# Other orders at three places of a hybrid decoder layer: a token norm and two weight splits, the rows of W_out, and a transpose's bank

## The chip, the cores and the metric

The kernel runs on one core of one Trainium2 chip. The time is the device time of one execution in microseconds (us); lower is better. Several executions are taken of each kernel, and their median counts. One more execution is recorded by the hardware profiler; all views of the trace come from it.

The engines are named as in the profile: PE is the matrix engine (TensorE; PEld its weight loads), DVE is VectorE, ACT is ScalarE, POOL is GpSimd, and SP issues the loads and stores. L1265 is line 1265 of the kernel.

## The reference

One decoder layer on 1024 tokens of width 1024 in float32, with 16 learned meta tokens ahead of them (so L = 1040 positions). The mixer has two groups of heads side by side, a state-space part (SSD) and a stick-breaking attention; a gated feed-forward part with a short convolution follows. Cut to what matters here:

```python
proj = rms_norm(h, mix_pre_g) @ w_in             # z, xbc (X, B, C), dt, q, k, v
y_ssd = ssd_mixer(z, xbc, dt_raw, ...)           # uses B and C, chunk by chunk
# stick breaking, per head: beta = sigmoid(q.k / 8)
w = beta[t, s] * prod(1 - beta[t, j] for s < j < t)
y_sb = rms_norm(w @ v, sb_norm_g)
mix = concatenate([y_ssd, y_sb], -1) @ w_out
h = h + rms_norm(mix, mix_post_g)
gu = rms_norm(h, ffn_pre_g) @ w_up               # g and u, 2816 columns each
f = (gelu(causal_dwconv(gu[..., :D_FF])) * gu[..., D_FF:]) @ w_down
h = h + rms_norm(f, ffn_post_g)
```

## The kernel before

**Products.** A float32 product is made of three: each operand is split into a rounded high part (`hi`, an ACT copy to `F32R`) and the rest (`lo`, a subtraction on POOL or DVE), and hi x hi, lo x hi and hi x lo are added up in PSUM. The order of the three differs: where weights are split against x (`plain`, L1336) it is weight-hi with x-hi, weight-hi with x-lo, then weight-lo with x-hi.

**Stages.** First the input norm, the projections and the SSD scan. Then the attention, eight pairs of heads `p` with eight blocks `i` of 128 queries; between its pieces PE gets the remaining projections and, at the end, the first half of W_out's product, as filling. Then the second half of W_out's product, token block by token block, with each block's two norms. Then the feed-forward products (`Problem`; `g0` and `u0` are the first two), in a scheme with seven products for eight, and last the product with W_down.

**What sets the order.** Outside of marked regions a planner orders each engine's instructions by its own estimates when the program is built; a region `manual_schedule` keeps the order of the code for the engines it names. Through the attention only PE is in such a region, so ACT, DVE, POOL and SP are the planner's there. From the second token block of W_out's second half to the end, PE, DVE, ACT and POOL all keep the order of the code (`ORDERED`), and SP is the planner's. `tc.issue_after(ins)` adds an edge of order alone: what its block emits on `ins`'s engine comes behind `ins` there. Tiles of one tag share a number of buffers (`bufs`), and a new tile waits until a buffer of its tag is free.

**Attention, one block (p, i).** `block_weights` (L752) computes the scores in chunks: PE writes a chunk to a tile `zz` (z), ACT reads it twice, into `kp` (L773) and `bt` (L774), both by a sigmoid. DVE scans `kp` (L780), POOL multiplies it into `bt` (L782). Two blocks later `block_turn` turns `bt` with PE (tw, L794), also into a tile `zz`, and ACT copies that to `th` (L796); `block_mix` (L809) is the product with v. There are two `zz` buffers for z and tw together. The loop gives PE the order: z, mix of an earlier block, filling, the turn of a block two back, filling.

**W_out's rows.** `wout_steps` (L888) prepares eight rows of W_out's first half, one per call: the raw row is loaded (tag `wraw`, two buffers), ACT copies it with a gain to the high part (`woa`, L894), DVE makes the rest (L895). `STAGE` says how many rows are to be there after block (p, i): one after (6,2), and one more per block up to eight after (7,1); the room for them comes from the projected x as the last projections end. `split_y` (L945) splits a block of the SSD's output the same way (yh on ACT, L951; yl, L952). In the trace, row six stands ahead of the score copies of block (6,6), though its call is at the end of block (6,7); the eight rows run from 776.5 to 822.8 us.

**B in token order.** `to_tokens` (L472) turns a 128-channel strip of X or B to token order in three parts: part 0 has the 16 meta tokens, parts 1 and 2 have four blocks of 128 each. Each part is written to a `tp` bank and copied out by DVE. There are two `tp` banks in this stage, and two `sd` banks, which the SSD scan uses.

**The last token block.** `after` (L1160) is the pair of norms of one token block, a generator with four stops: Square on ACT (L1162) and the root on POOL (ms, rs, L191 and L192) | scale and residual on DVE (L1165, L1166) and a store | second Square (L1171) | second root | and at its end the normed block `oxn` (DVE, L1175), which PE turns (x2tp, L1181). For block 8 the stops are spread by hand over the first feed-forward products. Their operands are g0's and u0's weights: `split_w` (L1262) splits a raw tile into `whi` (ACT, L1264) and `wlo` (POOL, L1265). PE's order there is: g0's first strip with x's first half (`ga_`) | x2tp of block 7 | `ga_`'s second half | g0's second strip with the first half (`gb_`, operands `whi2g` and `wlo2g`) | u0's first strip (`ua_`) | x2tp of block 8 | `gb_`'s second half | the rest.

The calls that the change touches there, before it:

```python
        elif t == NT:                      # L1511, ahead of the loop's end
            g0_pair = pair_w("2g0")
            u0.split_1()
            g0.split_2(g0_pair)
            load_raw(1, 1, wp, "wraw", 2)
...
    ga_ = g0_first(0, ("a11", "a12"))      # L1566
    run(ga_, 1)
    run(norm, 2)
    split_b22(nc.vector)
    turn7 = turn_x2(7, P, xn7, x2_tiles(7))
```

Of the kernel before, what the change touches and what calls it, by code (L numbers as in the profile page):

```python
# [9 lines left out]
F32 = mybir.dt.float32  # L10
F32R = mybir.dt.float32r
BF16 = mybir.dt.bfloat16
AF = mybir.ActivationFunctionType
ALU = mybir.AluOpType
# [3 lines left out]
P = 128  # L18
# [13 lines left out]
QSCALE = 0.125  # L32
# [9 lines left out]
WB = 3  # L42
# [11 lines left out]
def tile_layer(ctx: ExitStack, tc: tile.TileContext, x, meta, rows, parts,  # L54
               w_z, w_xbc, w_dt, w_q, w_k, w_v, w_out, w_up, w_down, out):
    nc = tc.nc
# [3 lines left out]
    wp = ctx.enter_context(tc.tile_pool(name="weights", bufs=2, side="left"))  # L60
# [13 lines left out]
    def psum_sd(name):  # L74
        return stage[0][1].tile([P, 512], F32, tag="sd", name=name, bufs=2)
# [10 lines left out]
    def psum_tp(name):  # L86
        return stage[0][1].tile([P, 4, P], F32, tag="tp", name=name, bufs=tp_bufs[0])
# [82 lines left out]
    def run(steps, n=None):  # L170
        for _ in steps if n is None else zip(range(n), steps):
            pass
# [55 lines left out]
    with tc.tile_pool(name="pre", bufs=3, side="right") as pre, \  # L228
# [21 lines left out]
        raws = {"B0": raw_of("B0", w_xbc[8])}  # L250
# [62 lines left out]
        for i in range(NT + 1):  # L313
# [7 lines left out]
            if i == 1:  # L321
                hl = wp.tile([P, KB, 32], F32R, tag="whi", name="wh_dt", bufs=WB)
# [42 lines left out]
    left = [0, 0]  # L365
# [87 lines left out]
    with tc.tile_pool(name="ssd", bufs=1, side="right") as sp:  # L453
# [17 lines left out]

        def to_tokens(src, dst, nm):  # L472
            for part in range(3):
                tp = psum_tp(f"tt_{nm}_{part}")
                if part == 0:
                    nc.tensor.transpose(tp[:NM, 0, :], src[:, 0:NM], ident)
                    nc.vector.tensor_copy(dst[:NM, 0, :], tp[:NM, 0, :])
                else:
                    for b in range(4):
                        t = 4 * (part - 1) + b  # L480
                        nc.tensor.transpose(tp[:, b, :], src[:, NM + t * P:NM + (t + 1) * P], ident)
                    nc.vector.tensor_copy(dst[:, 1 + 4 * (part - 1):5 + 4 * (part - 1), :], tp)
# [269 lines left out]
    def block_weights(p, i):  # L752
        kh, kl = heads[p][1]
        nm = f"{p}_{i}"
        if (p, i) not in qsplit:
            split_q(p, i)
        qh, ql = qsplit.pop((p, i))
        if i == 0:
            edges[p] = ap.tile([P, 2, NT, NM], F32, tag="cb", name=f"cb{p}", bufs=2)
            nc.gpsimd.memset(edges[p][:, :, :, NM - 1:], 0.0)  # L760
        n = NM + (i + 1) * P
        kpt = ap.tile([P, 2, L], F32, tag="kp", name=f"kp{nm}", bufs=2)
        btt = ap.tile([P, 2, L], F32, tag="bt", name=f"bt{nm}", bufs=3)
        kp, bt = kpt[:, :, 0:n], btt[:, :, 0:n]
        chunks = key_chunks(n)
        for ci, (a, w) in enumerate(chunks):
            if ci == 2:
                yield
            z = psum_zz(f"z{nm}_{ci}")
            for s_, (u, r) in enumerate(((qh, kh), (ql, kh), (qh, kl))):  # L770
                for h, j in zip(halves, range(2)):
                    mm(z[:, j, :w], u[h, :], r[h, a:a + w], start=s_ == 0, stop=s_ == 2)  # L772
            nc.scalar.activation(kp[:, :, a:a + w], z[:, :, :w], AF.Sigmoid, scale=-QSCALE)  # L773
            nc.scalar.activation(bt[:, :, a:a + w], z[:, :, :w], AF.Sigmoid, scale=QSCALE)  # L774
        nxt = (p, i + 1) if i < NT - 1 else (p + 1, 0)
        if nxt[0] in heads:
            split_q(*nxt)
        m = n - NM
        for j in range(2):
            nc.vector.tensor_tensor_scan(kp[:, j][:, ::-1], kp[:, j][:, ::-1], hold[:, L - n:L][:, ::-1], 0.0,  # L780
                                         op0=ALU.mult, op1=ALU.max)
            nc.gpsimd.tensor_tensor(bt[:, j, 0:m], bt[:, j, 0:m], kp[:, j, 1:m + 1], op=ALU.mult)  # L782
        nc.gpsimd.tensor_tensor(edges[p][:, :, i, 0:NM - 1], bt[:, :, m:n - 1], kp[:, :, m + 1:n], op=ALU.mult)
        turn.append((p, i, bt))
# [160 lines left out]
    def split_y(pool, half, t, tags, yk=None, eng=nc.gpsimd):  # L945
        nm = f"{half}_{t}"
        if yk is None:
            yk = load_y(half, t, yraw[0](f"yk{nm}"))
        yh = pool.tile([P, 8, P], F32R, tag=tags[0], name=f"yh{nm}", bufs=tags[2])
        yl = pool.tile([P, 8, P], F32R, tag=tags[1], name=f"yl{nm}", bufs=tags[2])  # L950
        nc.scalar.activation(yh, yk, AF.Copy)  # L951
        eng.tensor_tensor(yl, yk, yh.bitcast(F32), op=ALU.subtract)  # L952
        return yh, yl
# [43 lines left out]
    meta_steps = attend_meta()  # L997
    first = wsteps = None
    ys1 = []
    pe_order = ExitStack()  # L1000
    pe_order.enter_context(tc.manual_schedule(engines={mybir.EngineType.PE}))
    FILL = (3, 2, 1, 1, 1, 1, 1, 0)
    STAGE = {(6, 2): 1, (6, 3): 2, (6, 4): 3, (6, 5): 4, (6, 6): 5, (6, 7): 6, (7, 0): 7, (7, 1): 8}
    for p in range(8):
        for i in range(NT):
            if p == 0 and i == 0:
                run(fill, 1)
            block = block_weights(p, i)
            next(block, None)
            if mix:  # L1010
                block_mix(*mix.pop(0))
            if p > 0 and p != 6 and i == 3:
                edge_mix(p - 1, edge)
            run(fill, 1 + (i < FILL[p]))
            if p == 6 and i == 3:
                edge_mix(p - 1, edge)
            if first:
                run(first, 1)
            run(block)
            if (p, i) == (7, 1):  # L1020
                halo = halo_rows(ap, 0, y0a, wres, psum_mm("halo0"))
                run(halo, 3)
            ahead = iter(())
            if len(turn) > 2:
                ahead = begin_turn()
            if (p, i) == (7, 1):
                run(halo, 2)
            if i < NT - 1:
                run(ahead)
            run(fill, int(p > 0 or i > 3))  # L1030
            if (p, i) == (7, NT - 1):
                run(first, 1)
            run(ahead)
            if left[0] and wsteps is None:
                wres = []
                wsteps = wout_steps(third_slots(), 0, ssd_g, wres, [])
                y0a = halo_y(ap, 0)
            if (p, i) == (6, 3):
                yk = [load_y(0, 1, rp.tile([P, L + 3], F32, tag="rq", name="yk0_1", bufs=3)[:, :D]
                             .rearrange("p (a b) -> p a b", b=P)),  # L1040
                      load_y(0, 2, rp.tile([P, L], F32R, tag="rk", name="yk0_2", bufs=3).bitcast(F32)[:, :D]
                             .rearrange("p (a b) -> p a b", b=P))]
            if left[1] and not ys1:
                ys1.append(split_y(wp, 0, 1, ("whi", "wlo", WB), yk[0], nc.vector))
            if p > 0 and i == 2:
                edge = edge_turn(p - 1)
            for _ in range(2):
                if wsteps and len(wres) < min(8, 3 * left[0], STAGE.get((p, i), 0)):
                    run(wsteps, 1)
            if wsteps and first is None and len(wres) == 8:  # L1050
                run(wsteps)
                first = ssd_half(wres, ys1)
                run(first, 1)
                ys1.append(split_y(wp, 0, 2, ("whi", "wlo", WB), yk[1], nc.vector))
            elif first:
                run(halo)
                run(first, 1)
            if p == 7 and 2 < i < 6:
                run(meta_steps, 1)
            if p == 0 and i == 2:  # L1060
                token_rstd(r_ssd, ap, "a")
# [190 lines left out]
    raws = {}  # L1252

    def load_raw(j, gu, pool, tag, bufs):
        r = pool.tile([P, KB, P], F32, tag=tag, name=f"wr{gu}{j}", bufs=bufs)
        nc.sync.dma_start(out=r, in_=w_up[j, gu])
        raws[gu, j] = r

    def pair_w(nm):
        return [wp.tile([P, KB, P], F32R, tag=f"w{e}", name=f"w{e}{nm}", bufs=WB) for e in ("hi", "lo")]  # L1260
# [205 lines left out]
    for t in range(1, NT + 1):  # L1466
# [41 lines left out]
        if t == 7:  # L1508
            g0.split_1()
            load_raw(0, 1, wp, "wraw", 2)  # L1510
        elif t == NT:  # L1511
            g0_pair = pair_w("2g0")
            u0.split_1()
            g0.split_2(g0_pair)
            load_raw(1, 1, wp, "wraw", 2)
        run(steps)
        if t == 6:
            edge_x2()
# [41 lines left out]
    def g0_first(jj, ws):  # L1560
        g = f1.tile([P, 4, 258], F32, tag="gr", name=f"gr0_{jj}", bufs=2)
        g0.g.append(g)
        ghalf.append((g[:, 0:2, :], g[:, 2:4, :]))
        return g0.first_half(ws, psum_fa(f"g0{ws[0]}"), ghalf[jj], part_g)

    ga_ = g0_first(0, ("a11", "a12"))  # L1566
    run(ga_, 1)
    run(norm, 2)
    split_b22(nc.vector)
    turn7 = turn_x2(7, P, xn7, x2_tiles(7))  # L1570
    run(turn7, 1)
    run(norm, 1)
    xn8 = f1.tile([P, 1032], F32, tag="fa", name="oxn8")[:, :D]
    run(norm, 1)
    run(ga_)
    last_norm[0] = xn8
    run(norm)
# [333 lines left out]
```

## Time and profile before

| | us |
|---|---|
| median of 3 executions | 1728.21 (1726.89, 1728.21, 1728.25) |
| the profiled execution's own time | 1726.21 |
| its span, first to last instruction | 1724.3 |
| PE busy in the span | 1703.0 |
| POOL / DVE / ACT busy | 850.4 / 1117.8 / 821.2 |
| mean granted clock of PE | 0.998 |

How to read the views. A timeline row has the start and the duration in us, the engine, the line, the operation, output <- inputs, their shapes and types, how many instructions are merged in it (x1), and in brackets the idle time of the engine ahead of it with what ended that. A row of waits has who waited for whom, the total in us, how often, and the longest. A row of windows has the window, its length, PE's busy time with the instructions begun in it, the granted clock as a share of full speed, the share of the DMA engines and the GB/s. Starts and ends of matmuls overlap, as they are pipelined. A wait for several things is put down to the one that came last by the profile; where that engine had long been done, it was another.

### The profile page before, as it was taken

Reading aid. Unit: us, or ns where it says so; the run is one execution under the profiler, and the core shown is the slowest. Engines: PE = TensorE matmul, PEld = TensorE weight load, DVE = VectorE, ACT = ScalarE, POOL = GpSimd, SP = SyncE. Lnnn points to the kernel's source line nnn. Section 1 sums busy time; section 2 is a strip of 40 time slices with the busy share of each in tenths; the row PEclk is TensorE's granted clock in tenths of the full one; section 3 lists DMA queues with packets and bytes.
Section 4 is the critical chain, followed back from the end, with each engine's and each line's share of the span. In section 5 each row is a group of like instructions: output and inputs, shape, how many; then the busy total and the mean of one; then the engine's idle time right before and its main releaser. Section 6 shows DMA issues by size and latency. Waiting matters only on the chain. (4 is left out here: it accounts for less than half of the span.)

```text
span 1724.3 us, 28047 instructions
## 1 busy us (share of the span) xinstructions
PE 1703.0 (99%) x11230; PEld 1496.2 (87%) x11230; DVE 1117.8 (65%) x1233; ACT 821.2 (48%) x1370; POOL 850.4 (49%) x642
## 2 busy tenths in 40 slices
PE   7999999999999999999999999999999999999998
PEld 6999889888999998998788788999888888887886
DVE  5752973875676677578530567676666666658777
ACT  5423663555566566557652344433333333344544
POOL 4323664585566575565552122587767777400001
PEclk9999999999999999999999999999999999999999
DMA  4233343231011101112214653233332223395334
GB/s 164 58 111 98 105 127 108 68 105 38 26 38 38 36 28 38 38 50 86 64 68 147 212 174 123 73 107 110 103 92 92 92 92 99 118 330 180 105 113 179
DMA packets 90674, 173.87 MB, mean 101 GB/s; under 512 B 10704, under 2 KB 35816, under 8 KB 90544
## 3 DMA queue, kind: packets, MB, share of 16 engines
q1 hardware_dynamic: 90544, 172.08, 31.4%
q8 instruction: 88, 1.44, 0.4%
q14 instruction: 42, 0.34, 0.1%
HBM read 122.32 MB, written 49.73 MB: 100 GB/s over the span
## 5 line engine op out<-in xcount | busy, mean ns | idle before, releaser
L782 POOL TENSOR_TENSOR bt<-bt,kp 128x256 f32<-128x256 f32 (+7 forms) x128 | 213.0, 1683 | 185.7 <-DVE kp L780 144.3
L780 DVE TENSOR_TENSOR_SCAN kp<-kp,hold 128x272 f32<-128x272 f32 (+7 forms) x128 | 183.5, 1474 | 24.7 <-ACT kp L773 14.3
L1265 POOL TENSOR_TENSOR wlo<-wr,whi 128x1024 fp32r<-128x1024 f32 x43 | 107.7, 2516 | 37.8 <-ACT whi L1264 37.8
L1768 POOL TENSOR_TENSOR fms<-fms 128x1 f32<-128x1 f32 x8 | 2.6, 331 | 223.8 <-ACT dh L1653 197.1
L773 ACT ACTIVATE kp<-z 128x288 f32<-128x288 f32 (+6 forms) x112 | 82.6, 737 | 50.5 <-PE z L772 27.8
L1264 ACT ACTIVATE whi<-wr 128x1024 fp32r<-128x1024 f32 x43 | 45.6, 1060 | 111.5 <-PE fX L1322 67.9
L165 PE MATMUL pj_k<-xs,wh_k 128*128 128x400 f32 (+2 forms) x384 | 95.6, 336 | 0.0
L165 PE MATMUL pj_v<-xs,wh_v 128*128 128x400 f32 (+2 forms) x384 | 95.0, 334 | 0.0
L1394 DVE SCALAR_TENSOR_TENSOR ga<-gr,pp,ga 128x1024 f32<-128x1024 f32 x44 | 71.8, 1632 | 35.1 <-ACT ga L1387 34.3
L165 PE MATMUL pj_q<-xs,wh_q 128*128 128x386 f32 (+2 forms) x384 | 93.8, 331 | 0.0
L796 ACT ACTIVATE th<-tw 128x1024 f32<-128x1024 f32 (+2 forms) x96 | 75.6, 815 | 37.4 <-PE tw L794 37.3
L1653 ACT ACTIVATE dh<-ar 128x512 fp32r<-128x512 f32 x77 | 48.6, 631 | 92.9 <-PE dnB L1731 44.7
L165 PE MATMUL pj_X<-xs,wh_X 128*128 128x400 f32 (+2 forms) x384 | 92.0, 326 | 0.0
L165 PE MATMUL pj_z<-xs,wh_z 128*128 128x386 f32 (+2 forms) x384 | 91.6, 326 | 0.0
L748 DVE CAST qh<-q 128x128 fp32r<-128x128 f32 x64 | 45.5, 712 | 69.9 <-PE z L772 69.6
L1654 DVE TENSOR_TENSOR dl<-ar,dh 128x512 fp32r<-128x512 f32 x77 | 53.2, 691 | 50.2 <-ACT dh L1653 50.2
L966 PE MATMUL mo<-woa,yh 128*128 128x512 f32 x256 | 85.2, 400 | 0.0
L774 ACT ACTIVATE bt<-z 128x288 f32<-128x288 f32 (+6 forms) x112 | 82.9, 740 | 0.0
L794 PE MATMUL tw<-ident,bt 128*128 128x128 f32 x576 | 75.9, 274 | 2.2 <-POOL bt L782 1.6
L809 PE MATMUL av<-th,v 128*64 128x128 f32 x1152 | 77.2, 278 | 0.0
L809 PEld LDWEIGHTS av<-th,v 128*64 128x64 f32 x1152 | 61.5, 136 | 13.8 <-issue 10.9
L794 PEld LDWEIGHTS tw<-ident,bt 128*128 128x128 f32 x576 | 65.5, 141 | 8.6 <-issue 4.0
(560 smaller groups left out, 5623.9 us busy)
## 6 DMA issues: line engine op xcount, KB each, us to landing
wr<-in_w_up SPq DMA_DIRECT2D x44, 512.0 KB
fds<-ga SPq DMA_DIRECT2D x44, 256.0 KB
b<-in_w_down SPq DMA_DIRECT2D x44, 256.0 KB
ar<-fds SPq DMA_DIRECT2D x44, 256.0 KB
fda<-ga SPq DMA_DIRECT2D x33, 256.0 KB
ar<-fda SPq DMA_DIRECT2D x33, 256.0 KB
yk<-yd SPq DMA_DIRECT2D x16, 512.0 KB
wor<-in_w_out SPq DMA_DIRECT2D x12, 512.0 KB
```

Of the source, the lines that this page charges most:

```text
L165: mm(acc[:ncol, :n - s], a[:, k, :ncol], xs[c0][:, b, k, s:n], start=(k == 0 and j == 0), stop=(k == KB - 1 and j == 2))
L773: nc.scalar.activation(kp[:, :, a:a + w], z[:, :, :w], AF.Sigmoid, scale=-QSCALE)
L774: nc.scalar.activation(bt[:, :, a:a + w], z[:, :, :w], AF.Sigmoid, scale=QSCALE)
L780: nc.vector.tensor_tensor_scan(kp[:, j][:, ::-1], kp[:, j][:, ::-1], hold[:, L - n:L][:, ::-1], 0.0, op0=ALU.mult, op1=ALU.max)
L782: nc.gpsimd.tensor_tensor(bt[:, j, 0:m], bt[:, j, 0:m], kp[:, j, 1:m + 1], op=ALU.mult)
L794: nc.tensor.transpose(tw[:, j, b, :], bt[:, j, c0:c0 + P], ident)
L796: nc.scalar.activation(th[:, :, :nb, :], tw[:, :, :nb, :], AF.Copy)
L809: mm(av[halves[j], :], v[:, kb, halves[j]], th[:, j, b, :], start=kb == 0, stop=kb == i)
L966: recent[0] = mm(acc, u[:, k, :], v[:, cs], start=(k == 0 and j == 0), stop=(k == 7 and j == 2))
L1265: nc.gpsimd.tensor_tensor(l, raw, h.bitcast(F32), op=ALU.subtract)
L1394: nc.vector.scalar_tensor_tensor(v, self.g[jj][:, :, i:i + 256], fconv_w[:, j, i:i + 1], v, op0=ALU.mult, op1=ALU.add)
L1654: sub(lo[:, k], raw, hi[:, k].bitcast(F32), op=ALU.subtract)
```

## The change

Three edits. No arithmetic is changed, and no instruction is added or left out.

1. In `to_tokens`, part 0 of B's second strip ("B1") is written to an `sd` bank; the other parts and strips keep `tp`.
2. In the attention loop, `copied[0]` holds the last `bt` copy (L774) that was emitted. Each call for a row of W_out is wrapped in `issue_after(copied[0])`, and so is the split of y for token block 1, which is now made at block (6, 6) instead of when the last projections have begun their last chunk. The split of y for block 2 is not wrapped.
3. At the last token block, u0's split and g0's second split are taken apart. u0's ACT copy stays where both splits were; its POOL subtraction (`low_part`) comes behind the norm's first root. g0's ACT copy comes behind the norm's scale and residual; its POOL subtraction comes behind the norm's second root, and the load of u0's second raw tile with it. The first stop of the norm is now ahead of `ga_`. u0's pair of tiles is asked for ahead of g0's.

```diff
         def to_tokens(src, dst, nm):
             for part in range(3):
-                tp = psum_tp(f"tt_{nm}_{part}")
+                if part == 0 and nm == "B1":
+                    tp = psum_sd(f"tt_{nm}_0").rearrange("p (a b) -> p a b", b=P)
+                else:
+                    tp = psum_tp(f"tt_{nm}_{part}")
...
-            nc.scalar.activation(bt[:, :, a:a + w], z[:, :, :w], AF.Sigmoid, scale=QSCALE)
+            copied[0] = nc.scalar.activation(bt[:, :, a:a + w], z[:, :, :w], AF.Sigmoid, scale=QSCALE).ins
...
+    copied = [None]
...
-            if left[1] and not ys1:
-                ys1.append(split_y(wp, 0, 1, ("whi", "wlo", WB), yk[0], nc.vector))
+            if (p, i) == (6, 6):
+                with tc.issue_after(copied[0]):
+                    ys1.append(split_y(wp, 0, 1, ("whi", "wlo", WB), yk[0], nc.vector))
...
                 if wsteps and len(wres) < min(8, 3 * left[0], STAGE.get((p, i), 0)):
-                    run(wsteps, 1)
+                    with tc.issue_after(copied[0]):
+                        run(wsteps, 1)
...
         elif t == NT:
-            g0_pair = pair_w("2g0")
-            u0.split_1()
-            g0.split_2(g0_pair)
-            load_raw(1, 1, wp, "wraw", 2)
+            u0_pair, g0_pair = pair_w("1u0"), pair_w("2g0")
+            nc.scalar.activation(u0_pair[0], raws[1, 0], AF.Copy)
...
+    def low_part(raw, hl):
+        nc.gpsimd.tensor_tensor(hl[1], raw, hl[0].bitcast(F32), op=ALU.subtract)
+        return [(hl[0][:, s], hl[1][:, s]) for s in (LO4, HI4)]
+
+    run(norm, 1)
+    u0.w["a11"], u0.w["a12"] = low_part(raws[1, 0], u0_pair)
     ga_ = g0_first(0, ("a11", "a12"))
     run(ga_, 1)
-    run(norm, 2)
+    run(norm, 1)
+    nc.scalar.activation(g0_pair[0], raws[0, 1], AF.Copy)
     split_b22(nc.vector)
     turn7 = turn_x2(7, P, xn7, x2_tiles(7))
     run(turn7, 1)
     run(norm, 1)
     xn8 = f1.tile([P, 1032], F32, tag="fa", name="oxn8")[:, :D]
     run(norm, 1)
+    g0.w["a21"], g0.w["a22"] = low_part(raws[0, 1], g0_pair)
+    load_raw(1, 1, wp, "wraw", 2)
     run(ga_)
     last_norm[0] = xn8
     run(norm)
```

## The prediction

> **What bounds the kernel now.** I read the page's busy table first, then what TensorE (PE) waits for, then each of these waits in the timelines of the engines around it, and last the granted clock in short windows.
>
> ```profile
> span 1724.3 us, 28047 instructions
> PE 1703.0 (99%) x11230; PEld 1496.2 (87%) x11230; DVE 1117.8 (65%) x1233; ACT 821.2 (48%) x1370; POOL 850.4 (49%) x642
> ```
>
> PE is busy 99% of the span, so an edit pays only where PE stands still or runs at a lower clock. The waits of PE, each with its total, its count and its longest:
>
> ```profile
> PE tw L794 <- POOL bt L782: 1.6, 1, 1.6
> PE x2tp L1181 <- DVE oxn L1175: 1.4, 1, 1.4
> PE tw L794 <- ACT bt L774: 0.5, 1, 0.5
> PE tt_B L481 <- DVE bn L477: 0.5, 1, 0.5
> ```
>
> The three edits stand at just these four waits, 4.0 us in all. Two windows hold what the waits do to the clock (window, length, PE busy, granted clock, DMA):
>
> ```profile
> 807.19:810.60 3.41, 1.23 (x10) 1.00 0.62 167
> 810.60:814.01 3.41, 3.41 (x16) 0.50 0.38 141
> ...
> 1070.01:1073.42 3.41, 1.99 (x17) 1.00 0.30 74
> ```
>
> A stretch with 1.23 us busy of 3.41 (36%) is followed by one of equal length at half clock; one with 1.99 (58%) is not. The price of half a clock is in the spacing of equal matmuls:
>
> ```profile
> 806.26 0.28 PE L165 MATMUL pj_k<-xs,wl_k 128*128 128x256 f32 x1
> 806.62 0.28 PE L165 MATMUL pj_k<-xs,wl_k 128*128 128x256 f32 x1
> ...
> 812.00 0.41 PE L165 MATMUL pj_k<-xs,wl_k 128*128 128x256 f32 x1
> 812.64 0.41 PE L165 MATMUL pj_k<-xs,wl_k 128*128 128x256 f32 x1
> ```
>
> 0.64 us in place of 0.36: one stretch of 3.41 us costs 3.41 x (1 - 0.36/0.64) = 1.5 us.
>
> **Part 1, W_out's rows behind the scores' copies.** At block (6,6):
>
> ```profile
> 803.58 0.37 PE L772 MATMUL z<-kl,qh 64*128 64x456 f32 x2
> ...
> 808.90 1.06 PE L794 MATMUL tw<-ident,bt 128*128 128x128 f32 x8 [1.65 <-POOL bt L782]
> 810.50 0.64 PE L794 MATMUL tw<-ident,bt 128*128 128x128 f32 x2 [0.53 <-ACT bt L774]
> ```
>
> ```profile
> 804.80 1.15 ACT L894 ACTIVATE woa<-wor,pp 128x1024 fp32r<-128x1024 f32 x1 [1.13 <-DMA wor<-in_w_out]
> 805.86 0.36 ACT L382 ACTIVATE q<-pj_q 128x256 f32<-128x256 f32 x1
> 806.12 1.05 ACT L951 ACTIVATE yh<-yk 128x1024 fp32r<-128x1024 f32 x1
> 807.07 0.92 ACT L773 ACTIVATE kp<-z 128x912 f32<-128x912 f32 x1
> 807.88 0.93 ACT L774 ACTIVATE bt<-z 128x912 f32<-128x912 f32 x1
> ```
>
> The first z chunk is in PSUM at 803.58 + 0.37 = 803.95. ACT reads it at 807.07, because a W_out row (which waits 1.13 us for its load) and a y split stand ahead. z and tw share two buffers, and the first turn starts at 808.90, 0.09 after bt ends (808.81): the row names POOL, but what freed the bank was ACT's bt. With both behind the last bt of their own block, kp can start 3.1 us earlier, and bt ends at 805.7, before PE comes to tw at 808.90 - 1.65 = 807.25. Both waits go (1.65 + 0.53 = 2.18), and with them the half clock: **-3.7**. The margin of 1.5 us covers one more copy of 1.15, not two. What is moved now stands ahead of th: row and y split (1.15 + 1.05) behind a bt that ends near 807.3 can hold th until 809.5, and the next z wants th's bank (1.05 later, 810.6) at about 813.63 - 3.7 = 809.9; a new wait of 0 to 0.7. I take 0. The rows' loads move too, since a raw tile comes free a block later; but one row per block of some 7 us is slower than the load:
>
> ```profile
> 800.05 9.64 SPq L882 DMA_DIRECT2D wor<-in_w_out  x3
> ```
>
> The first of these starts at 800.05 and the row that waits for its load runs at 804.80: 4.75 us. Bounds: -4.0 to -2.9; if the copies only collide elsewhere, 0.
>
> **Part 2, first rows of B in another bank.**
>
> ```profile
> 310.40 0.27 DVE L477 COPY bn<-tt_B 16x128 f32<-16x128 f32 x1
> ...
> 310.72 0.66 PE L481 MATMUL tt_B<-ident,bt 128*128 128x128 f32 x4 [0.47 <-DVE bn L477]
> ```
>
> The third group of turns needs the bank that DVE empties late, behind a convolution step. With part 0 in the idle `sd` bank, it takes the other `tp` bank: **-0.5**. No instruction is added; bounds -0.5 and 0 (the next user of the bank waits instead).
>
> **Part 3, the last norm ahead of the weight splits.** The rows of POOL, DVE, ACT and PE, in this order:
>
> ```profile
> 1059.48 2.39 POOL L1265 TENSOR_TENSOR wlo<-wr,whi 128x1024 fp32r<-128x1024 f32 x1 [1.90 <-ACT whi L1264]
> 1061.83 2.84 POOL L1265 TENSOR_TENSOR wlo2g<-wr,whi2g 128x1024 fp32r<-128x1024 f32 x1
> ...
> 1069.56 0.22 POOL L191 TENSOR_SCALAR ms_ff<-oss 128x1 f32<-128x1 f32 x1 [3.93 <-ACT t4l L1171]
> 1069.87 0.57 POOL L192 TENSOR_TENSOR rs_ff<-ms_ff,nhalf 128x1 f32<-128x1 f32 x1
> ```
>
> ```profile
> 1058.93 0.75 DVE L1478 SCALAR_TENSOR_TENSOR mb<-mo,r_sb,mb 128x512 f32<-128x512 f32 x1
> ...
> 1065.66 1.28 DVE L1165 SCALAR_TENSOR_TENSOR mb<-mb,rs_mo,gpost 128x1024 f32<-128x1024 f32 x1 [3.25 <-POOL rs_mo L192]
> 1066.98 1.23 DVE L1166 TENSOR_TENSOR mb<-mb,xr 128x1024 f32<-128x1024 f32 x1
> ...
> 1070.47 1.28 DVE L1175 SCALAR_TENSOR_TENSOR oxn<-mb,rs_ff,gffn 128x1024 f32<-128x1024 f32 x1 [0.44 <-POOL rs_ff L192]
> ```
>
> ```profile
> 1068.32 1.06 ACT L1171 ACTIVATE t4l<-mb 128x1024 fp32r<-128x1024 f32 x1 [4.11 <-DVE mb L1166]
> ...
> 1084.26 1.06 ACT L1264 ACTIVATE whi<-wr 128x1024 fp32r<-128x1024 f32 x1 [2.34 <-PE g0c L1336]
> ```
>
> ```profile
> 1064.92 0.28 PE L1336 MATMUL g0a<-b11h,wlo2g 128*128 128x258 f32 x1
> ...
> 1070.08 0.40 PE L1336 MATMUL u0a<-b11h,wlo 128*128 128x512 f32 x1
> 1071.90 1.06 PE L1181 MATMUL x2tp<-ident,oxn 128*128 128x128 f32 x8 [1.42 <-DVE oxn L1175]
> ```
>
> Today both splits run first on POOL, the norm's two roots follow, and oxn is 1.42 late for PE. But PE's order is not touched: it multiplies with wlo2g at 1064.92, 0.25 us after POOL has written it (1061.83 + 2.84), long before x2tp. The edit puts this split behind the norm's second root. So I follow the new chain. Evacuation ends at 1059.68; Square 0.1 later, and 1.24 (1068.32 to 1069.56) to ms, 0.88 to the root's end (1069.87 + 0.57): 1061.9. Now u0's split takes POOL and L1165 wants DVE at once. How such a race goes is shown early in the trace:
>
> ```profile
> 20.23 1.28 POOL L304 TENSOR_TENSOR wl_B<-wr_B,wh_B 128x512 fp32r<-128x512 f32 x1
> ...
> 20.29 2.30 DVE L273 SCALAR_TENSOR_TENSOR xn<-xt,rs_pre,gpre 128x1024 f32<-128x1024 f32 x1 [0.47 <-POOL rs_pre L192]
> ```
>
> POOL starts 0.06 ahead, and a DVE instruction of 1.28 takes 2.30 and ends 1.08 after POOL: one waits for the other. So u0's split runs to 1064.25, L1165 to 1065.35, L1166 to 1066.6; Square and root again (0.1 + 1.24 + 0.88): 1068.8; g0's split of 2.39: 1071.2. The wlo2g matmul moves from 1064.92 to 1071.2: 6.3 us. x2tp then waits no more (oxn ends near 1072.3, PE needs it near 1071.2 + 5.6 = 1076.8), so 1.42 comes back: **+4.9**. Bounds of the wait: 4.1, if DVE keeps the way for L1165 and L1166 (1061.9 + 2.5 + 2.2 + 2.39 = 1069.0), and 7.6, if oxn goes ahead of g0's split at the end. Behind PE's waiting matmul stand u0a, x2tp and all that follows.
>
> A PE gap of 6 us holds at least one window under 36% busy, so half clock follows: one stretch, **+1.5**, between 0.8 (PE comes back in the middle of it) and 2.3 (one and a half stretches). The load of u0's second raw tile moves behind g0's split, to about 1071; with the 4.75 us above it lands near 1076, hidden behind the work up to 1084.26, where ACT first reads it; without that cover it would cost these 4.75.
>
> [...]
>
> **The sum.** -3.7 - 0.5 + 4.9 + 1.5 = +2.2 us. On the profiled execution (span 1724.3, its own time 1726.21) that is 1728.4. The three other runs lie at 1726.89, 1728.21 and 1728.25, so the profiled one is 2.0 under their median; on the mean of all four, 1727.4, I get **1729.6 us**. About 0.2% (3.5 us) is what can be told from no change.
>
> **Rivals.**
> 1. Slower, at part 1: the planner orders ACT anew, and row plus y split ahead of th hold back a later z as long as today. For it: ACT has little room there, and row 6 and the y split took 2.2 us at once. Against: one row per block. Then -3.7 is lost: +5.9, 1733.3. It decides once part 1 gives less than 2.4.
> 2. At the final root DVE is first: oxn ahead of g0's split, +1.3: 1730.9. The row at 20.23 speaks against it.
> 3. DVE keeps the way for both L1165 and L1166: wait 4.1, sum 0.0: 1727.4. Against it, the same row.
> 4. The change does other than its text says: the ordered region lets g0's split stand ahead, or PE's order moves; no wait of 6 us, -3.7 - 0.5 - 1.4 = -5.6: 1721.8, faster. Against: POOL ran the steps in the code's order before.
> 5. u0's pair is now asked for before g0's. If the three slots are taken in turn, the next pair waits for u0c's end in place of g0d's, 5.6 us later, and POOL's chain to the next product has no slack: about +5 more, 1734.6. No row tells how slots are chosen.
>
> **Chances.** Forecast 0.47 (own range 1727.5 to 1731.8, from the bounds of clock and new wait), rivals 0.22, 0.10, 0.08, 0.07, 0.06. Slower by over 0.2%: 0.07 of the forecast, 0.20 of the first, 0.05 of the second, 0.06 of the fifth: 0.38. Faster: the fourth and 0.01 of the forecast, 0.08. Within: 0.54. The range 1725.0 to 1734.5 leaves out the fourth, part of the fifth and the ends of the first.
>
> **What would show it.** Part 1: no PE wait at tw L794 of 0.5 or more between 780 and 830, granted clock 1.00 there, kp at (6,6) within 0.5 of its z. Part 2: no tt_B wait. Part 3: a PE wait of about 6 us at g0a for POOL's wlo2g, none at x2tp, ms and rs on POOL ahead of either split, and clock 0.50 for some 3.4 us behind it. No such wait at g0a would make the prediction wrong, as would a new wait over 1 us in the attention stage.

## The result and the profile after

| kernel | median of its runs, us | ratio to before, 95% interval |
|---|---|---|
| before | 1727.17 (1725.41 to 1728.25) | |
| changed | 1742.29 (1739.39 to 1743.92) | 1.0086 [1.0074, 1.0097] |

The change costs 15 us. The forecast was 1729.6 in a range of 1725.0 to 1734.5, so it is wrong: the measured time lies 7.8 us above the top of the range. The first lines of the page of the changed kernel, whose profiled execution took 1742.29 us:

```profile
span 1740.6 us, 28044 instructions
PE 1709.3 (98%) x11230; PEld 1501.6 (86%) x11230; DVE 1124.2 (65%) x1233; ACT 821.5 (47%) x1370; POOL 854.0 (49%) x642
```

PE stands idle for 1740.6 - 1709.3 = 31.3 us, against 21.3 before: +10.0. It is also busy 6.3 us longer with the same 11230 products, so part of them ran at a lower clock: its mean granted clock is 0.993, before's 0.998. What PE waits for (total, count, longest), the rows of the changed places:

```profile
PE g0a L1342 <- POOL wlo2g L1571: 6.5, 1, 6.5
PE z L775 <- ACT th L799: 4.5, 4, 2.1
PE sg L627 <- ACT sgh L618: 1.9, 2, 1.4
PE vtp L419 <- ACT v L420: 0.5, 1, 0.5
```

All four waits of before that the prediction lists (two at tw, one at x2tp, one at tt_B) are gone, as forecast. Each place has a larger one in their stead: 6.5 for 1.4 at the last norm, 5.0 for 2.1 in attention, 1.9 for 0.5 near B. Together that is +9.4 of the +10.0. The prediction named a new wait of over 1 us in the attention stage as a sign that it was wrong; two came (1.24 and 2.12, below).

**At the last norm** the chain ran as forecast. POOL, then VectorE (DVE), then PE in the timeline:

```profile
1070.71 0.57 POOL L192 TENSOR_TENSOR rs_mo<-ms_mo,nhalf 128x1 f32<-128x1 f32 x1
1071.24 2.42 POOL L1571 TENSOR_TENSOR wlo1u<-wr,whi1u 128x1024 fp32r<-128x1024 f32 x1
...
1078.19 2.35 POOL L1571 TENSOR_TENSOR wlo2g<-wr,whi2g 128x1024 fp32r<-128x1024 f32 x1
...
1071.31 3.43 DVE L1171 SCALAR_TENSOR_TENSOR mb<-mb,rs_mo,gpost 128x1024 f32<-128x1024 f32 x1 [0.77 <-POOL rs_mo L192]
...
1078.26 3.37 DVE L1181 SCALAR_TENSOR_TENSOR oxn<-mb,rs_ff,gffn 128x1024 f32<-128x1024 f32 x1 [0.45 <-POOL rs_ff L192]
...
1080.60 0.58 PE L1342 MATMUL g0a<-b11h,wlo2g 128*128 128x258 f32 x1 [6.47 <-POOL wlo2g L1571]
```

POOL starts at 1071.24, DVE 0.07 later, and DVE's 1.28 us become 3.43: it ends 1.08 after POOL, as in the row at 20.23 that the prediction went by. The same happens at the second root: oxn starts 0.07 after g0's split and takes 3.37 in place of 1.28. The wait of 6.47 is the 6.3 of the forecast. The windows behind it (window, length, busy time of PE, PEld, DVE, ACT, POOL, granted clock, DMA share, GB/s):

```profile
1074.86:1078.27 3.41, 0.00 (x0) 0.00 (x0) 2.96 (x5) 2.15 (x4) 0.83 (x3) 1.00 0.75 282
1078.27:1081.68 3.41, 1.08 (x5) 1.08 (x6) 3.41 (x2) 0.96 (x2) 2.27 (x1) 0.51 0.17 25
1081.68:1085.10 3.42, 3.42 (x18) 3.42 (x18) 2.29 (x3) 0.00 (x0) 0.00 (x0) 0.50 0.78 264
```

Two windows at half clock, one of them mostly idle. At the forecast's price of 0.64 for 0.36 they cost (1.08 + 3.42) x 0.44 = 2.0 us, an estimate.

**Near B** nothing but PE moved, and that was enough. Before, DVE and POOL:

```profile
314.07 1.52 DVE L468 SCALAR_TENSOR_TENSOR ct<-craw_C,pp,ct 128x256 f32<-128x256 f32 x3
...
315.74 1.90 POOL L617 TENSOR_TENSOR sgl<-tri,adl 128x1024 fp32r<-128x1024 f32 x1 [1.87 <-PE sg L624]
```

After, DVE, POOL, ACT and PE:

```profile
314.00 3.19 DVE L468 SCALAR_TENSOR_TENSOR ct<-craw_C,pp,ct 128x256 f32<-128x256 f32 x3
...
315.01 1.90 POOL L620 TENSOR_TENSOR sgl<-tri,adl 128x1024 fp32r<-128x1024 f32 x1 [1.19 <-PE sg L627]
...
317.23 0.42 ACT L470 ACTIVATE ct<-ct 128x256 f32<-128x256 f32 x1 [4.78 <-DVE ct L468]
...
320.88 0.50 PE L627 MATMUL sg<-sgh,lowr 128*128 128x512 f32 x1 [1.44 <-ACT sgh L618]
```

POOL's split of chunk 1 waits for PE's small sg products of chunk 0. Before, it starts at 315.74, 0.15 after DVE's three steps end (314.07 + 1.52 = 315.59). With the change PE is there 0.7 earlier (the wait at tt_B is gone), POOL starts at 315.01 in the middle of them, and the steps take 3.19 in place of 1.52. ACT needs their result first, q and sgh stand behind it in ACT's queue, and PE's next sg waits for sgh. The 0.5 us that PE gained bought a wait of 1.9. Half clock (granted 0.50) follows in the window from 323.97 to 327.39; in the one ahead of it, which has the end of this wait in it, PE is busy for 2.66 us of 3.41.

**In attention** there are four new waits, with three causes. The first, DVE, ACT and PE:

```profile
792.81 2.05 DVE L898 SCALAR_TENSOR_TENSOR woa<-wor,pp,woa 128x1024 fp32r<-128x1024 f32 x1
794.78 0.41 DVE L835 TENSOR_TENSOR ysc<-avc,ysc 128x256 f32<-128x256 f32 x1
...
795.29 1.06 ACT L842 ACTIVATE sqb<-ysc 128x1024 f32<-128x1024 f32 x1 [3.20 <-DVE ysc L835]
796.25 0.58 ACT L799 ACTIVATE th<-tw 128x512 f32<-128x512 f32 x1
...
796.88 0.41 PE L775 MATMUL z<-kh,qh 64*128 64x328 f32 x2 [1.24 <-ACT th L799]
```

A W_out row has two halves, a copy on ACT and a low pass on DVE. The later copy put the low pass between the scan and ysc. ACT's sqb waits for ysc, th stands behind sqb, and z wants the bank of th. The second:

```profile
813.64 1.09 ACT L954 ACTIVATE yh<-yk 128x1024 fp32r<-128x1024 f32 x1
814.59 1.18 ACT L897 ACTIVATE woa<-wor,pp 128x1024 fp32r<-128x1024 f32 x1
815.63 1.32 ACT L799 ACTIVATE th<-tw 128x1024 f32<-128x1024 f32 x2
...
816.74 0.43 PE L775 MATMUL z<-kh,qh 64*128 64x348 f32 x2 [0.90 <-ACT th L799]
```

This is the collision that the prediction's part 1 weighed ("a new wait of 0 to 0.7. I take 0"). The other two, of 0.26 at z (with 0.53 at vtp) and 2.12 at z, come from loads. SP's queue of before, then that of after with DVE, ACT and PE:

```profile
828.89 2.03 SPq L942 DMA_DIRECT2D yk<-yd  x2
```

```profile
804.30 28.65 SPq L885 DMA_DIRECT2D wor<-in_w_out  x4
...
837.34 7.34 SPq L945 DMA_DIRECT2D yk<-yd  x3
...
835.80 1.50 DVE L898 SCALAR_TENSOR_TENSOR woa<-wor,pp,woa 128x1024 fp32r<-128x1024 f32 x1
...
827.12 1.15 ACT L897 ACTIVATE woa<-wor,pp 128x1024 fp32r<-128x1024 f32 x1 [0.90 <-DMA wor<-in_w_out]
...
840.84 1.06 ACT L954 ACTIVATE yh<-yk 128x1024 fp32r<-128x1024 f32 x1 [2.85 <-DMA yk<-yd]
841.80 1.92 ACT L799 ACTIVATE th<-tw 128x1024 f32<-128x1024 f32 x2
...
842.86 0.70 PE L775 MATMUL z<-kh,qh 64*128 64x400 f32 x2 [2.12 <-ACT th L799]
```

The rows' low passes end later, so their raw tiles come free later, and the last four row loads stretch from 804.30 to 832.95. The load of y stands behind them on SP and goes to the same ring of raw tiles: it is issued at 837.34, 0.04 after a row's low pass ends (835.80 + 1.50), in place of 828.89, while PE itself is only 3.6 us later there (its turns stood at 830.36 and stand at 833.97). ACT's yh waits for it, th waits behind yh. Half clock follows this wait too, 0.50 from 842.80 to 846.21.

**Two windows at half clock have no wait ahead of them**, 0.50 from 419.55 to 422.96 and from 948.61 to 952.02. Windows of the changed kernel, and PE's row in them:

```profile
415.83:419.25 3.42, 3.42 (x29) 3.16 (x29) 1.24 (x3) 0.78 (x2) 2.41 (x3) 1.00 0.56 158
419.25:422.66 3.41, 3.41 (x21) 2.85 (x22) 1.69 (x5) 2.29 (x5) 1.83 (x1) 0.54 0.00 0
```

```profile
417.09 2.07 PE L445 MATMUL pta<-ones,sq 128*2 128x1 f32 x18
```

PE counts as busy for all of the first window, but 2.07 us of it are 18 products of a single column. A like run, ptb, stands at 946.42, and one of 16 products of four columns (avm, 1.94 us) at 882.42. Before has the same three runs and no half clock behind any: its granted clock is 1.00 from 15.29 to 810.59 and from 814.01 to 1721.93. Whether this belongs to the change is one of the questions for the runs.

### The profile page after: what moved, and what is told of

The parts are those of the page before. It is cut to its first block, busy times and chain, and to the rows that moved or that the text cites. A ratio compares the mean times of both kernels' runs of the same rounds, so it can differ in the third digit from the quotient of the medians.

```text
span 1740.6 us, 28044 instructions
## 1 busy us (share of the span) xinstructions
PE 1709.3 (98%) x11230; PEld 1501.6 (86%) x11230; DVE 1124.2 (65%) x1233; ACT 821.5 (47%) x1370; POOL 854.0 (49%) x642
## 5 line engine op out<-in xcount | busy, mean ns | idle before, releaser
L785 POOL TENSOR_TENSOR bt<-bt,kp 128x256 f32<-128x256 f32 (+7 forms) x128 | 217.1, 1715 | 183.7 <-DVE kp L783 145.5
```

## Experiments

Every kernel is shown by its edit, or by the part of the diff above that it takes. They ran in three groups: the first four; `b_p1r`, `b_p1s`, `b_p2dve` and `tiny`; and the last four. Each group was timed against the kernel before, run beside it, with a median of 1727.36, 1726.91 and 1726.62 us. A ratio is worked out from all executions and is not the quotient of two medians; the two differ by up to 0.08%.

### Each part alone, and the order of the splits

`b_p1`, `b_p2` and `b_p3` are the kernel before with the part of that number of the diff above and nothing else. `b_p3m` is `b_p3` with the two low splits exchanged, and the ACT copies that they need with them:

```diff
-            nc.scalar.activation(u0_pair[0], raws[1, 0], AF.Copy)
+            nc.scalar.activation(g0_pair[0], raws[0, 1], AF.Copy)
...
     run(norm, 1)
-    u0.w["a11"], u0.w["a12"] = low_part(raws[1, 0], u0_pair)
+    g0.w["a21"], g0.w["a22"] = low_part(raws[0, 1], g0_pair)
...
     run(norm, 1)
-    nc.scalar.activation(g0_pair[0], raws[0, 1], AF.Copy)
+    nc.scalar.activation(u0_pair[0], raws[1, 0], AF.Copy)
...
-    g0.w["a21"], g0.w["a22"] = low_part(raws[0, 1], g0_pair)
+    u0.w["a11"], u0.w["a12"] = low_part(raws[1, 0], u0_pair)
```

Part 1:

> Kernel before with part 1 alone (y split and W_out rows behind the score copies). Theory A (the copies collide elsewhere, in four places of their own: a row's low pass on VectorE ahead of the edge sum, a row and a y split ahead of th, a row that waits for its load ahead of v, and a y load issued late): PE waits of about 5 us for th and v between 770 and 870 in place of the 2.18 us of waits at tw, and one half-clock stretch as before: +2 to +4 us on the kernel before. Theory B (these waits come from PE arriving at another time because of part 2): the tw waits go, no wait over 0.7 us takes their place: -2 to -4 us.

Part 2:

> Kernel before with part 2 alone (first rows of B in the sd bank). [...] Theory B (as forecast, and the wait near 321 in the changed kernel is chance or comes from another part): no wait for sgh, -0.5 us.

Part 3:

> Kernel before with part 3 alone (last norm ahead of the weight splits). Theory A: PE waits 6.3 to 6.7 us at g0a for wlo2g, none at x2tp, two stretches at half clock of which about 2 us are lost: +6 to +8 us. Theory B (the wait in the changed kernel is long because the whole kernel ran late before it): wait under 5 us, +3 us or less.

Splits exchanged:

> Kernel before with part 3, but with the two low splits exchanged: the one of g0 behind the first root, the one of u0 behind the second. Theory A (the loss is that PE needs wlo2g first and u0's low part 5.2 us later): no wait for wlo2g, a wait of 1 to 2.5 us at u0a or x2tp, no half clock behind it: 0 to +1.5 us on the kernel before. [...]

| kernel | median, us | ratio, interval | PE waits in its profile, us |
|---|---|---|---|
| b_p1 | 1730.53 | 1.0026 [1.0015, 1.0036] | z 4.1 (4), vtp 0.9, no tw |
| b_p2 | 1731.41 | 1.0026 [1.0016, 1.0036] | sg 1.9, no tt_B |
| b_p3 | 1734.17 | 1.0044 [1.0030, 1.0058] | g0a 6.5, no x2tp |
| b_p3m | 1730.57 | 1.0021 [1.0010, 1.0031] | u0a 3.4, no g0a, no x2tp |

The waits of the three parts stand at the same places as in the whole change: for parts 1 and 3 those of theory A, for part 2 the 1.9 at sg, where its theory B had none. The times are less exact. Part 3 lies in its expected +6 to +8. Part 1 is +3.2 us by the medians and +4.5 by the ratio, where +2 to +4 was expected; part 2 is +4.1 and +4.5, where theory B had -0.5. The profile of `b_p2` shows one reason to be careful with sizes: it has four windows at half clock ahead of its last 3 us, and only the one at 324 stands behind the wait at sg; the other three follow the runs of tiny products. The excesses add up: 0.26 + 0.26 + 0.44 = 0.96%, the whole change has 0.86 [0.74, 0.97]. In `b_p3m` the wait for wlo2g goes and a smaller one for u0's low part comes, 3.4 and not the 1 to 2.5 expected, and the time lies above the 0 to +1.5 us expected. So either split behind the second root is late for PE, g0's by more.

### Which of the moved copies does the harm

`b_p1r` moves the rows alone (the y split stays where it was before); `b_p1s` moves only the y split and the one row that stood ahead of kp at block (6,6). The edit of `b_p1s`:

```diff
-            if left[1] and not ys1:
-                ys1.append(split_y(wp, 0, 1, ("whi", "wlo", WB), yk[0], nc.vector))
+            if (p, i) == (6, 6):
+                with tc.issue_after(copied[0]):
+                    ys1.append(split_y(wp, 0, 1, ("whi", "wlo", WB), yk[0], nc.vector))
+                bt66 = copied[0]
...
-                    run(wsteps, 1)
+                    with tc.issue_after(bt66) if (p, i) == (6, 7) else ExitStack():
+                        run(wsteps, 1)
```

Rows alone:

> Kernel before with the W_out rows alone behind the score copies; the y split stays where the planner had it, ahead of kp at block (6,6). Theory A (the rows do the harm: each is a block later, so its low pass, its load and the y load behind it are late): the tw waits stay above 0.5 us or go, waits at z for th and at vtp of together 2.5 to 5 us appear: +2 to +4 us on the kernel before. Theory B (the y split in its new place ahead of th does it): at most 1 us of waits at z and vtp: -1 to +1 us.

Two copies:

> Kernel before with only the two copies that stood ahead of kp at block (6,6), the y split and one W_out row, put behind the score copies of that block; all other rows stay. Theory A (the idea of part 1 is right for these two, the other rows do the harm): no wait at tw between 780 and 830, at most 1 us at z, no half clock there: -2 to -4 us. Theory B (two copies ahead of th hold it as long as they held kp): a wait of 1.5 to 2.5 us at z in place of the one at tw, -0.5 to +1 us.

`b_p1r` takes 1732.24 us, 1.0028 [1.0018, 1.0038], with waits of 1.24, 0.17 and 2.02 at z and a new one of 1.58 at a later tw (831): the waits of theory A, so the rows do it, through their low passes and loads. The time, +5.3 us by the medians and +4.8 by the ratio, lies above the +2 to +4 expected; three windows at half clock behind the runs of tiny products stand in its profile. The 0.9 at z is not there; it needs the y split and a row ahead of one th. `b_p1s` takes 1728.22, 1.0007 [0.9997, 1.0017], neither theory. The waits of PE in it, and ACT's row ahead of the first:

```profile
PE tw L794 <- ACT bt L774: 1.4, 1, 1.4
PE z L772 <- ACT th L796: 1.1, 2, 0.9
```

```profile
823.47 1.15 ACT L894 ACTIVATE woa<-wor,pp 128x1024 fp32r<-128x1024 f32 x1 [1.79 <-DMA wor<-in_w_out]
```

The wait at tw near 808 is gone as wanted, 0.9 of it came back at z, and a row further on now waits 1.79 for its load and holds bt. Even the smallest form of part 1 only moves about 2 us of waits and wins nothing.

The eight profiles in which this place has its old copy order (before, `b_p3`, `b_p3m`, `b_p2`, `b_p2dve`, `tiny`, `turn8`, `best0`) show that the prize was also smaller than the forecast's 2.18: the waits at tw there are 2.2, 2.3, 1.2, 1.0, 0.9, 1.0, 1.1 and 1.0 us. In the first two the row ahead of kp waits 1.13 and 1.28 for its load; in the other six it waits for none. Only these two have a half clock there.

### Who holds the step on ct

`b_p2dve` is `b_p2` with POOL's split of chunk 1 of the second group given to DVE. If that split, begun in the middle of DVE's steps on ct, is what stretches them from 1.52 to 3.19 us, they are short again here and the wait of 1.9 goes:

```diff
+            eng = nc.vector if (g, c) == (1, 1) else nc.gpsimd
-            nc.gpsimd.tensor_tensor(sgl[:nr, :, :nr], ...
+            eng.tensor_tensor(sgl[:nr, :, :nr], ...
```

> Kernel before with part 2, and the split sgl of chunk 1 of the second group moved from POOL to VectorE. [...] Theory B (the sd bank or PE's order delays ACT's sgh): a wait of over 1 us at sg stays.

1727.50 us, 1.0001 [0.9992, 1.0010]. DVE, and PE's wait:

```profile
313.89 1.53 DVE L468 SCALAR_TENSOR_TENSOR ct<-craw_C,pp,ct 128x256 f32<-128x256 f32 x3
```

```profile
PE sg L628 <- ACT sgh L618: 0.4, 1, 0.4
```

Without POOL's split in the way the three steps take 1.53 again, the wait of 1.9 is gone, and no half clock follows (equal products still start 0.36 us apart from 322.55 to 325.05): POOL's split was the cause, and theory B does not hold. The -0.5 that part 2 was forecast to give does not come: ACT's chain did not get earlier, and the 0.5 saved at tt_B stands at sg as 0.4. So in this order part 2 had nothing to win even without the collision.

### The runs of tiny products

`tiny` is the kernel before with these runs cut up; `a_tiny` is the changed kernel with the same cuts. The core of the edit (avm likewise in two pieces):

```diff
+        for g in range(3):
+            pt = psum_mm(f"pt{nm}{g}")
+            for t in range(3 * g, 3 * g + 3):
+                a, nr = (M0, 2) if t == 0 else (NM + (t - 1) * P, P)
+                mm(pt[:nr, t:t + 1], sq[:, a:a + nr], ones[:, 0:1], start=True, stop=True)
...
+            yield
```

Cut in before:

> Kernel before with the three runs of tiny products (2.07 us of 18 one-column products twice, 1.94 us of 16 four-column products once) cut into three, three and two pieces with other products between. Theory A (a clock window of 3.41 us into which one of these runs falls whole is followed by one at half clock, and where the windows lie differs from execution to execution): no half clock at these places in any profile, median 1.5 to 3 us under the kernel before, and a spread under 3.5 us where before has 5. Theory B (these half-clock stretches come from somewhere else): they stay, and the time is within 0.7 us of before.

Cut in the changed kernel:

> The changed kernel with the three runs of tiny products cut into pieces, as in the kernel tiny. Theory A (the change costs what its own three places cost: about 5 us of wait and 2 of clock at g0a, 3 to 4.5 in attention, 1.4 to 3 near 321): 12 to 14.5 us above tiny, so 1736 to 1739, with no half clock behind the pieces. Theory B (a good part of the change's loss is that it shifts the tiny products into worse places of the clock windows): under 11 us above tiny, 1735 or less.

`tiny` takes 1724.08 us (1723.91 to 1725.34), 0.9983 [0.9974, 0.9993]: faster than both kernels, with no half clock in its profile after the start but in the last 3 us, and with a spread of 1.4 us over 10 executions, where before, run beside it, has 6.9 over 31 (1723.65 to 1730.55). Theory A. `a_tiny` takes 1738.79 us, inside the 1736 to 1739 of theory A, and 14.7 above `tiny`, where theory A had 12 to 14.5; it has no half clock behind the pieces either. So the runs of tiny products cost the kernel before about 3 us (2.8 by the medians, 1.2 to 4.5 by the interval of the ratio), and the change's loss is not theirs. What they cost the changed kernel is not settled: 3.5 us by the medians, which are of different groups, 0.11% (1.9 us) by the ratios, whose intervals overlap.

### A way round the wait at x2tp

The gain that part 3 was after is 1.4 us at x2tp. `turn8` leaves norm and splits alone and gives PE other work first; `best0` adds it to `tiny`, and `best1` also the y split alone behind the score copies:

```diff
+    run(gb_)
     run(turn8, 1)
     run(turn8, 1)
-    run(gb_)
```

turn8:

> Kernel before with the turns x2tp of the last token block moved on PE behind the second half of the g0 product that stood behind them; all splits and the norm stay. Theory A (PE only needs other work of 2.9 us ahead of the turns): no wait at x2tp, none over 0.5 us behind it, -1.4 us. Theory B (the wait moves to the products that use the turned block): a wait of over 1 us at g0c or u0a, within 0.5 us of before.

best0:

> Kernel before with the tiny products cut and the turns x2tp moved behind the g0 product. Theory A (the two gains add up): 1.3 to 1.6 us under tiny, 1722.2 to 1723.2, that is 0.2 to 0.3% under before. Theory B (the wait at x2tp comes back elsewhere): within 0.5 us of tiny.

best1:

> The kernel best0 with the y split alone (no W_out row) behind the score copies of block (6,6). Theory A (this one copy held kp, and th has room for it): the waits at tw near 808 fall from about 1 us to 0.5 or less and no new wait over 0.3 comes at z: 0.5 to 1 us under best0. Theory B (ACT has no room there at all, as with the two copies): a wait of 0.5 to 1 us at z for th, 0 to +0.7 us on best0.

1729.91 (1.0025 [1.0015, 1.0036]), 1725.53 (1.0001 [0.9992, 1.0009]) and 1726.60 (1.0001 [0.9992, 1.0010]). None helps, no theory A of the three holds, and `tiny` stays the fastest. `turn8`, PE's wait and ACT's rows:

```profile
PE g0a L1336 <- ACT gr L1342: 2.1, 1, 2.1
```

```profile
1068.82 1.57 ACT L1223 ACTIVATE t1h<-xa 128x1032 fp32r<-128x1032 f32 x2
1070.87 0.60 ACT L1342 ACTIVATE gr<-g0a 128x516 f32<-128x516 f32 x1 [0.47 <-DVE oxn L1175]
```

The g0 product that was moved ahead adds to a bank whose first half ACT must read out first. That read stands behind two splits, and behind them it waits 0.47 more for oxn, the very block that PE was to wait for no longer. The code shows the link: the read writes a tile of tag `gr`, which has two buffers, and the norm's block mb, from which oxn is made, is of that tag (L1474). In `best0` and `best1` the same read waits 0.53 for the store of mb. The wait of 1.4 became 2.1, at neither of the two places named, and in some executions a half clock follows it (there is one in the profiles of `turn8` and `best1`, none in that of `best0`). `best1` ends at 0.5 at tw for bt, 0.7 at tw without a releaser in the profile, and 0.4 in two waits at z. In its profile the row ahead of kp waits 1.09 for its load, so kp starts at 805.66, hardly earlier than the 805.85 of `best0`; whether the copy had room is not shown.

## Why the prediction was wrong, step by step

**What bounds the kernel.** Right: PE waits and clock windows explain the result (idle +10.0 us, busy +6.3). But the list of waits was read as a list of gains. In the change the four waits went, and at each of the three places a larger one came.

**Part 1, forecast -3.7, measured +3.2 by the medians, +4.5 by the ratio (0.0026 of 1727 us).** The step that failed is "what is moved now stands ahead of th [...] I take 0", with "slower than the load" behind it. The move was costed as ACT copies at one block. Left out were the rows' low passes on DVE (1.24 us of wait), the SP queue behind the rows, on which y's load came 8.5 us later (2.12), and a copy that waits for its load ahead of v (0.8). The 0 to 0.7 for th was 0.9. The removal itself was right: no wait at tw, but 2.18 and a half clock belong to two of eight profiles; the other six have 0.9 to 1.2 and no half clock. The profile of `b_p1` accounts for +3.0 us of span: PE idle for 24.4 us against 21.3, busy for 1702.9 against 1703.0. The first rival had the right mechanism at 0.22, but took for its worst that the gain is merely lost.

**Part 2, forecast -0.5, measured +4.1 by the medians, +4.5 by the ratio.** The step that failed is "bounds -0.5 and 0 (the next user of the bank waits instead)". It looked for a loss at the bank alone, and did not ask what PE, once earlier, releases: POOL's split at 315.74 started 0.15 behind DVE's steps. The prediction had read that very collision of POOL and DVE for part 3. Of the time, 1.4 is the wait (1.9 for 0.5) and about 1.5, by the forecast's price, the window at half clock behind it. This 2.9 lies at the low end of the interval of the ratio (2.8 to 6.2 us); what the rest is stays open.

**Part 3, forecast +4.9 and +1.5, measured alone +6.8 by the medians, +7.6 by the ratio (5.2 to 10.0).** Right, mechanism and size. The wait is 6.5 for 6.3, POOL and DVE went as in the early race, x2tp's wait is gone, and the clock cost an estimated 2.0, in its bounds of 0.8 to 2.3. The rule for the clock was too coarse, though. It was read from two windows, 36% busy (half clock follows) and 58% (none); in `b_p3m` windows of 53% and 48% have none behind them, and near 323 of the changed kernel one of 78% has.

**The other rivals.** DVE ahead at the last root did not happen (POOL starts wlo2g at 1078.19, oxn starts at 1078.26), nor did DVE keeping the way for both steps, and the wait of 6 us came. Rival 5 (a slot freed later) did not show: no later PE wait is larger than before.

**The sum.** With parts 1 and 2 at +4.5 each and part 3 at +7.6 the same addition gives +16.6, where the whole has 14.9 (12.8 to 16.8); by the medians it is +14.1 for +15.1. The form of the sum was sound. Two terms had the wrong sign, and their bounds did not reach past zero.

## What to carry to other kernels

A wait in a kernel that is 99% busy on one engine can be a point where two chains meet; before crediting its removal, follow what the earlier engine then releases, and check whether that now runs into something on another engine that it used to stand just behind. A copy that moves carries its low pass, the tile it frees, the load into that tile and everything behind that load in the queue; bound each with a loss, not with zero. And cut long runs of one-column products into pieces between full ones: here this gained about 3 us, and no reordering gained any.

## What the runs showed of the hardware

**Half clock followed 17 of 30 runs of tiny products.** In the changed kernel five stretches at 0.50 begin at 323.97, 419.55, 842.80, 948.61 and 1078.32, 28, 124, 31 and 38 times 3.413 us apart to within 0.04; each is 3.41 us long, the last 6.83. So windows of 3.41 us, laid end to end from a half-clock window of each profile, give the window in which each of the three runs starts. Over ten profiles with uncut runs (before, changed, b_p1, b_p1r, b_p1s, b_p2, b_p2dve, b_p3, b_p3m, turn8):

| from the run's start to the end of that window | half clock in the next window |
|---|---|
| 2.05 to 3.33 us | 17 of 17 |
| 0.16 to 2.02 us | 0 of 13 |

PE is shown as busy throughout. The windows lie elsewhere in each profile (the first half-clock window, modulo 3.41 us, begins at 1.63 in before, 3.12 in the changed kernel, 0.44 in b_p3m), and a profile has between none and three of these stretches, at an estimated 1.5 us each by the spacing of equal products (0.64 for 0.36, before near 812 and 806). This is most of the spread: in the three groups, executions of before with a mean granted clock of 0.999 have spans of 1721.5 to 1724.5 us, those with 0.996 have 1725.6 to 1728.7, and 0.003 of the span is what three windows at half clock make (3 x 3.41 x 0.5 us of 1725). A run of 1.94 to 2.07 us of tiny products had half clock behind it, and so had a wait of 2.1 (`turn8`).

A longer wait had none behind it. The wait of 3.37 us in `b_p3m` falls over two windows, with PE busy for 1.81 and 1.65 us of 3.41, and no half clock follows. The waits of 2.1 to 2.2 us in `turn8`, `best1` and `best0` leave 1.30, 1.25 and 1.93 us busy in their window; half clock follows the first two and not the third. The window ahead of 323.97 in the changed kernel, busy for 2.66 us, does not fit a rule by busy time; why half clock follows it is not shown.

**Where POOL's split started 0.06 to 0.07 us ahead of DVE's step, DVE ended 1.08 to 1.09 us after POOL.** In before, at 20.23, POOL took 1.28 and DVE 2.30. In the changed kernel POOL took 2.42 at 1071.24 and DVE's step 3.43, which took 1.28 when alone (before, 1065.66); at 1078.19 POOL took 2.35 and oxn 3.37. Three short steps on ct took 3.19 for 1.52 when POOL's split of 1.90 started 1.01 after the first of them.
